# Alternating strides and three-step merges in a dilated attention kernel, with a stepwise memory stage

## The chip, the cores and the metric

The kernel runs on one core of one Trainium2 chip. The metric is device time in microseconds (us) of one launch. A core has TensorE (PE in the profile; PEld is its weight load), VectorE (DVE), ScalarE (ACT), GpSimd (POOL) and SyncE (SP, which here only issues DMAs). DMAs are issued from SP's queue (SPq) or ACT's (ACTq); both feed the same 16 DMA engines.

## The reference

A trunk of two layers over 1024 tokens of width 1024. Layer 0 is dilated sliding-window attention, layer 1 a gated linear recurrence; both also attend to 256 memory tokens. The change concerns layer 0:

```python
h = rms_norm(x, norm_gain[l])
cols = h @ w_in_a[j]                      # q, k, v of 3 groups x 8 heads, memory queries, gate
for g, (window, dil) in enumerate(((128, 1), (512, 4), (2048, 16))):
    o, lse = dilated_window_attention(q[:, :, g], k[:, :, g], v[:, :, g], dil, window // dil)
alpha = softmax(stack(lses), axis=0)      # per token and head, over the groups
mix = sum(alpha[..., None] * stack(outs), axis=0)
kv = rms_norm(mem, mem_gain) @ w_kv       # memory keys and values, both layers
mem_out = softmax(qm @ km^T * scale) @ vm # 4 heads
x = x + (concat([mix, mem_out]) * silu(gate)) @ w_out
```

## The kernel before, in words

Matrices are multiplied in float32 split in two parts: each weight piece (128 x 1024) is loaded as `raw`, then made into `wh` (ACT, rounded) and `wl` (DVE, the rest); a product is three matmuls (high x high, high x low, low x high) of 128 x 128 by 128 x 512. `piece` (L195) does load, high and low part of one piece in one go; `plan` lists all pieces in order, `ahead` prepares them, `take` hands them out. There are two `raw` buffers and four of each of `wh` and `wl`.

Order of the instructions on an engine: a planner orders them by a timing model, except inside `pinned()` (L150), which keeps the written order on the engines it names (TensorE by default). A queue or an engine then runs strictly in the order that the planner left.

Layer 0 runs in these stages:

- Prologue (L1055 to L1074). Four times a pair of x tiles is loaded, normalised, turned and split (`x_pair`), and a projection of gate chunk 0 follows. In the last round come `tables` (L761: sines and cosines of positions, a chain of some 45 small DVE instructions) and the first weight loads `load(0, ...)`, among them block "11"; after that the first split of weights.
- The big projection of q, k and v (`step`, L1037): 252 pinned steps of 12 matmuls, by a seven-product scheme with sums of quarter blocks. `emptied`, `spread`, `normed`, `flip` and `spill_heads` carry each result on over the next seven steps (`BEHIND` = 6) and write it to scratch memory (`qk_scr`, `v_scr`). Scratch rooms in SBUF are `m0` to `m3`, `u0` to `u3`, `w0` to `w3`.
- Its tail and gate slice 0 (L1081 to L1084), in the planner's order.
- Memory stage (L1123 to L1153). The memory tokens are loaded and normalised (`mem_norm`), gate slice 1 runs (`gate_mem`, L1128), the tokens are turned (`mem_turn`), `mem_kv` makes keys and values of both layers (four products of 48 matmuls), then `mem_queries` projects the queries tile by tile and `mem_attend` does scores, softmax and values for pairs of tiles.
- Attention (L1155 to L1277). `heads` lists 12 items (group g, pair of heads hp): four of g = 2 (stride 16), then g = 1 (stride 4), then g = 0 (stride 1). Each has eight steps m: `scores` (L1181 matmuls, L1184 DVE mask and minimum, L1186 ACT exponential with its sum), one step later `turn_` (L1195 transposes, `pts` copy), then `values` (L1208). A step has one key block (g = 2, m < 4 of g = 1, m = 0 of g = 0) or two. Every second step of g > 0 `spill` copies the result to `os` and stores it with two DMAs from ACT's queue (L1228); for g = 0 `merge` (L1231) loads the other two groups' results (`others`), works out the weights from minima and sums in `st`, and stores the weighted sum (L1253). `fetch` loads q, k and v of the next item (1 MB each) on SP's queue, two sets of buffers taking turns. One matmul of gate slices 2 and 3 (`gate_mem_steps`, L533) is put into each step as a filler.
- Gate chunk 1 covers the end of attention; the output projection and layer 1 follow.

At the top, L109 sets the queues: `LQ, SQ, WQ = Y, A, Y`, so loads and weights go by SP (`Y`) and stores by ACT (`A`).

Of the kernel before, what the change touches and what calls it, by code (L numbers as in the profile page):

```python
# [103 lines left out]
def trunk_kernel(ctx, tc, x, mem, pos, norm_gain, w_in_a, q_gain_a, k_gain_a, qk_gain_t, w_out_a,  # L104
# [90 lines left out]
    def piece(src, gain=None):  # L195


        a = src.shape[1]
        raw = rpool.tile([128, 1024], F32, name="raw")
        v = lambda t: t.rearrange("p (a b) -> p a b", a=a)  # L200
        WQ.dma_start(v(raw[:]), src)
# [7 lines left out]
        hi = pool.tile([128, 1024], F32R, name="wh")  # L209
        lo = pool.tile([128, 1024], F32R, name="wl")  # L210
        if gain:
            for b in range(a):
                g = gain()[:, b:b + 1]
                A.activation(v(hi[:])[:, b], v(raw[:])[:, b], AF.Copy, scale=g)
                V.scalar_tensor_tensor(v(lo[:])[:, b], v(raw[:])[:, b], g, v(hi[:])[:, b].bitcast(F32), op0=OP.mult, op1=OP.subtract)
            return v(hi[:]), v(lo[:])
        copy(W_HI, hi[:], raw[:])
        rests.append(W_LO.tensor_tensor(lo[:], raw[:], hi[:].bitcast(F32), op=OP.subtract).ins)  # L218
        return v(hi[:]), v(lo[:])
# [11 lines left out]
    at_piece = [0, 0]  # L231

    def ahead(n):

        while at_piece[1] < min(at_piece[0] + n, len(plan)):
            ready[at_piece[1]] = piece(*plan[at_piece[1]][1:])
            at_piece[1] += 1
# [85 lines left out]
    def mem_gains(pool, name):  # L323

        rows_ = pool.tile([16, 128], F32, name=name)
        Y.dma_start(rows_[:], mem_norm_gain.rearrange("l (k p) -> (l k) p", p=128))
        t = pT.tile([128, 4, 128], F32, name="pt")
        T.transpose(t[:, 0, 0:16], rows_[:], ident[0:16, 0:16])
        V.tensor_copy(memory[0], t[:, 0, 0:16])

    def mem_norm(pool):

        xns = []
        for m in range(2):
            xt = pool.tile([128, D], F32, name="xt")
            Y.dma_start(xt[:], mem[m * 128:(m + 1) * 128, :])
            xns.append(norm_rows(xt[:], None, D, pool))
        return xns

    def mem_turn(pool, xns):  # L340

        mts = []
        for xn in xns:
            hi = pool.tile([128, 8, 128], F32R, name="mhi")
            lo = pool.tile([128, 8, 128], F32R, name="mlo")
            transposed_split(xn, hi, lo, 8)
            mts.append((hi, lo))
        return mts

    def mem_kv(l, mts, pool, put_k, put_v):  # L350


        gt = pool.tile([128, 2], F32, name="mgt")
        Y.dma_start(gt[:], mem_gain_t[l])
        gk = pool.tile([128, 24], F32, name="mgk")
        V.tensor_tensor(gk[:, 0:1], gt[:, 0:1], gt[:, 1:2], op=OP.mult)
        for part in range(2):
            W = take(("mem", l, part), 4)
            pss = [pp.tile([128, 512], F32, name="acc") for _ in range(2)]
            project([ps[:] for ps in pss], [lambda k, t=t: (t[0][:, k, :], t[1][:, k, :]) for t in mts], W)  # L360
            for m, ps in enumerate(pss):
                if part:
                    put_v(m, ps[:])
                else:
                    put_k(m, heads_T(head_norm(ps[:], pool, bufs=1))[:], gk[:, 0:1])

    def mem_queries(key, km, vm, ppool, pool, prob, scr, lhs, before=lambda m: None, after=lambda hp: None):
# [4 lines left out]
        def each(m, ps):  # L372
            t = heads_T(head_norm(ps, pool))
            hi, lo = (pool.tile([128, 4, 128], F32R, name=n, bufs=4) for n in ("qmh", "qml"))
            split_evac(hi[:], lo[:], t[:])
            qs[m] = hi, lo
            before(m)
            if m > 1:
                mem_attend(m // 2 - 1, m % 2, qs, km, vm, ppool, pool, prob, scr)

        project_tiles(key, lhs, each)
        for hp in range(2):
            mem_attend(NT // 2 - 1, hp, qs, km, vm, ppool, pool, prob, scr)
            after(hp)

    def mem_attend(mp, hp, qs, km, vm, ppool, pool, prob, scr):

        ph, pl = (ppool.tile([128, 4, 256], F32R, name=n) for n in ("pmh", "pml"))
        for i in range(2):
# [17 lines left out]
            G.tensor_tensor(p, p, bc(den[:, :, None], [128, 2, MEM]), op=OP.mult)  # L407
            t = pT.tile([128, 4, 128], F32, name="pt")
# [4 lines left out]
            split_evac(ph[:, :, sl], pl[:, :, sl], t[:])  # L413
        o = pO.tile([128, 2, 256], F32, name="po")
# [10 lines left out]
        SQ.dma_start(scr[hp * 256:(hp + 1) * 256, mp * 256:(mp + 1) * 256].rearrange("(h p) t -> p h t", p=128), os[:])  # L425
# [99 lines left out]
    def gate_mem_steps(i):  # L525

        (wh, wl), = take(("gate_m", i), 1)
        for hf in range(2):
# [8 lines left out]
            SQ.dma_start(gatem_scr[i * 128:(i + 1) * 128, hf * 512:(hf + 1) * 512], sg)  # L537
        ahead(4)
# [91 lines left out]
    plan_slices(MG0)  # L630
# [5 lines left out]
    plan_slices(MG1)  # L636
# [101 lines left out]
    with ExitStack() as sa:  # L738
# [19 lines left out]
        def room(name, **kw):  # L758
            return wx.tile([128, 4, 128], F32, name=name, **kw)[:]

        def tables():  # L761

            posi = wx.tile([128, NT], I32, name="w1")
# [885 lines left out]
```

## Time and profile before

| | us |
|---|---|
| median of 3 runs (lowest, highest) | 2116.57 (2115.84, 2116.68) |
| profiled execution, its own time | 2117.12 |
| span of its instructions | 2115.3 |
| first attention scores to the end of attention | about 979 to 1184 |

The profile is of one execution. A line of a group gives the line of the kernel, engine, operation, output and inputs, shapes and count, then busy time, mean time of one, and the idle time of the engine before them with what ended it. A row of a stretch gives busy time per engine, the mean granted TensorE clock (1.00 is full), the share of time that the 16 DMA engines were busy (it can pass 1, since packets overlap) and GB/s. Matmuls are pipelined: the distance of two starts, not the length of one, is its cost.

### The profile page before, as it was taken

How to read it: one execution, taken by the hardware profiler on the slowest of the kernel's cores; microseconds unless marked ns; L12 is line 12 of the kernel's file. 1: busy time of each engine (PE TensorE's matmuls, PEld its weight loads, DVE VectorE, ACT ScalarE, POOL GpSimd, SP SyncE). 2: the span in 40 equal slices, each digit the busy share in tenths (PEclk: the TensorE clock that was granted, in tenths of full speed). 3: DMA queues.
4: the chain of work that ended last, by engine and by line, in shares of the span. 5: the costliest groups of instructions: out<-in, count | busy, mean ns of one | idle time of the engine just before them, and what ended most of it. 6: DMA issues, size and time to landing. Idle time of an engine off the chain costs nothing.

```text
span 2115.3 us, 29553 instructions
## 1 busy us (share of the span) xinstructions
PE 2054.5 (97%) x10713; PEld 1733.5 (82%) x10713; DVE 1242.4 (59%) x2457; ACT 863.1 (41%) x1635; POOL 533.6 (25%) x664
## 2 busy tenths in 40 slices
PE   7899999999999998998898999999999999999999
PEld 6688888888888886787787878888888888888887
DVE  6865566736766465555467554425477762776443
ACT  5454255633554344546566332224522222322220
POOL 3362065703754054122006400012200000000221
PEclk9999999999999999999999999999999999999999
DMA  6277479553544417525899474330301121113643
GB/s 200 93 135 115 130 134 116 120 164 93 119 122 140 130 50 246 185 60 199 276 297 281 147 256 150 125 113 25 100 26 56 57 63 40 51 60 95 234 126 113
DMA packets 418896, 277.21 MB, mean 131 GB/s; under 512 B 220592, under 2 KB 344768, under 8 KB 416704
## 3 DMA queue, kind: packets, MB, share of 16 engines
q1 hardware_dynamic: 379696, 232.20, 40.7%
q10 hardware_dynamic: 39056, 43.14, 5.8%
q8 instruction: 85, 1.39, 0.3%
q14 instruction: 59, 0.48, 0.1%
HBM read 192.32 MB, written 82.97 MB: 130 GB/s over the span
## 4 chain that ended last, share of the span: by engine, by line
PE 46%; DMA 5%; ACT 1%; DVE 1%; issue 0%; ACTq 0%; POOL 0%; SPq 0%; DVEq 0%
PE acc L498 5%; PE acc L499 5%; PE acc L500 5%; PE acc L603 4%; PE acc L604 4%; PE acc L605 4%; PE acc L258 3%; PE acc L256 3%; PE acc L257 3%; DMA o_scr<-os 3%; PE s L1404 1%; PE pt L1404 1%; PE s L1181 1%; PE po L1208 1%; ACT pa L1186 1%; PE pt L299 1%
## 5 line engine op out<-in xcount | busy, mean ns | idle before, releaser
L172 ACT ACTIVATE wh<-raw 128x1024 fp32r<-128x1024 f32 x206 | 216.6, 1054 | 187.0 <-PE acc L499 48.7
L181 POOL TENSOR_TENSOR rr<-rv,nhalf 128x4 f32<-128x4 f32 (+1 forms) x54 | 50.0, 926 | 759.4 <-DVE rv L179 750.9
L1001 POOL TENSOR_TENSOR rr<-rv,nhalf 128x4 f32<-128x4 f32 x96 | 125.0, 1302 | 412.2 <-DVE rv L999 411.0
L889 DVE TENSOR_TENSOR wl<-raw,wh 128x1024 fp32r<-128x1024 f32 x126 | 158.1, 1255 | 115.2 <-ACT wh L172 114.3
L500 PE MATMUL acc<-hhi,wl 128*128 128x512 f32 x480 | 191.4, 399 | 0.1
L498 PE MATMUL acc<-hhi,wh 128*128 128x512 f32 x480 | 190.3, 396 | 1.1 <-ACT wh L172 1.1
L499 PE MATMUL acc<-hlo,wh 128*128 128x512 f32 x480 | 191.3, 398 | 0.0
L218 DVE TENSOR_TENSOR wl<-raw,wh 128x1024 fp32r<-128x1024 f32 x80 | 99.3, 1243 | 131.8 <-ACT wh L172 131.1
L258 PE MATMUL acc<-wh,hlo 128*128 128x512 f32 x384 | 151.0, 394 | 4.9 <-DVE hlo L277 4.9
L256 PE MATMUL acc<-wh,hhi 128*128 128x512 f32 x384 | 150.4, 396 | 1.5 <-ACT wh L172 0.9
L257 PE MATMUL acc<-wl,hhi 128*128 128x512 f32 x384 | 151.0, 393 | 0.0
L603 PE MATMUL acc<-wh,yhi 128*128 128x512 f32 x360 | 142.6, 398 | 0.5 <-ACT yhi L172 0.5
L604 PE MATMUL acc<-wl,yhi 128*128 128x512 f32 x360 | 141.0, 392 | 0.0
L605 PE MATMUL acc<-wh,ylo 128*128 128x512 f32 x360 | 139.8, 393 | 0.0
L957 PE MATMUL acc<-wl,hhi 128*128 128x512 f32 x324 | 127.0, 392 | 4.5 <-DVE wl L889 4.5
L956 PE MATMUL acc<-wh,hhi 128*128 128x512 f32 x324 | 128.1, 395 | 1.6 <-ACT wh L172 1.6
L958 PE MATMUL acc<-wh,hlo 128*128 128x512 f32 x324 | 127.0, 392 | 0.0
L1186 ACT ACTIVATE pa<-pa,st 128x128 f32<-128x128 f32 (+1 forms) x192 | 84.5, 441 | 54.2 <-DVE st L1184 19.4
L498 PEld LDWEIGHTS acc<-hhi,wh 128*128 128x128 f32 x480 | 90.3, 188 | 18.3 <-ACT wh L172 1.6
L499 PEld LDWEIGHTS acc<-hlo,wh 128*128 128x128 f32 x480 | 90.3, 188 | 17.0
L500 PEld LDWEIGHTS acc<-hhi,wl 128*128 128x128 f32 x480 | 90.3, 188 | 16.8 <-DVE wl L218 0.3
L893 DVE TENSOR_TENSOR raw<-raw 128x1024 f32<-128x1024 f32 x72 | 90.2, 1260 | 16.4 <-DMA raw<-in_w_in_a_dram 16.4
(335 smaller groups left out, 5156.5 us busy)
## 6 DMA issues: line engine op xcount, KB each, us to landing
raw<-in_w_in_a_dram SPq DMA_DIRECT2D x115, 512.0 KB, 4.4
raw<-in_w_in_b_dram SPq DMA_DIRECT2D x40, 512.0 KB, 3.7
qk_scr<-m SPq DMA_DIRECT2D x48, 256.0 KB, 3.5
o_scr<-os ACTq DMA_DIRECT2D x96, 128.0 KB, 4.6
raw<-in_w_mem_kv_dram SPq DMA_DIRECT2D x16, 512.0 KB, 3.8
kT<-qk_scr SPq DMA_DIRECT2D x8, 1024.0 KB, 5.3
qT<-qk_scr SPq DMA_DIRECT2D x8, 1024.0 KB, 8.4
vv<-v_scr SPq DMA_DIRECT2D x8, 1024.0 KB, 7.3
```

The source lines that it names most:

```text
L172: A.activation(dst, src, AF.Copy)
L256: T.matmul(ps, hi, wh[:, j, :], start=at == 0, stop=False)
L257: T.matmul(ps, hi, wl[:, j, :], start=False, stop=False)
L258: T.matmul(ps, lo, wh[:, j, :], start=False, stop=at == n - 1)
L498: T.matmul(ps[:], wh[:, k, :], mh, start=k == 0, stop=False)
L499: T.matmul(ps[:], wh[:, k, :], ml, start=False, stop=False)
L500: T.matmul(ps[:], wl[:, k, :], mh, start=False, stop=k == 7)
L603: T.matmul(pss[ch][:], hi[:, k, :], wh[:, j, :], start=first and k == 0, stop=False)
L604: T.matmul(pss[ch][:], hi[:, k, :], wl[:, j, :], start=False, stop=False)
L605: T.matmul(pss[ch][:], lo[:, k, :], wh[:, j, :], start=False, stop=end and k == 3)
L889: V.tensor_tensor(lo[:], source(n, h), hi.bitcast(F32), op=OP.subtract)
L956: T.matmul(flat, hi, wh, start=kt == 0 and p in (0, 1, 5), stop=False, **on)
```

## The change

Four parts of layer 0 are rewritten; layer 1 only gets its memory functions cut up under new names. The arithmetic is the same, but for the merge, whose last product and sum become one instruction per head.

1. **Pieces in parts.** `piece` becomes `piece_raw`, `piece_hi`, `piece_lo`, with `load_piece` and `split_piece` to call them one at a time.
2. **Prologue.** `tables` and the loads of "11" stand ahead of the first gate projection. "11" goes to rooms of the projection's scratch that are unused then; for that, `u2`/`u3` and `w2`/`w3` become halves of one tile each, and `x_pair` uses `u0`, `u1`, `w0`, `w1` only.
3. **Memory stage.** Loads, norm and turning of the memory tokens, and loads and splits of the pieces needed, are put into the last steps of the big projection. Its eight tail steps, now with TensorE pinned, take 12 matmuls each of gate slice 0 and of the memory keys. The other three key/value products follow. Queries run in 13 pinned rounds; gate slice 1 moves from before the key/value products into the last five of them.
4. **Attention.** The items alternate; q and k are fetched two items ahead (three sets), v one ahead; fillers come three at a time in stride 16 alone; stores in attention and in the memory stage go by SP; the `os` buffers are three, in a pool of their own; `merge` is split into `weigh`, its `rest` and `merge`, which run in successive steps.

Its core:

```diff
@@ prologue
         W = take(("gate", 0), 4)
+        tables()
+        for h in range(2):
+            load(0, "11", h)
         for j in range(4):
...
-                tables()
...
-                for b, h in (("11", 0), ("11", 1), ("12", 0), ("12", 1), ("21", 0), ("21", 1), ("22", 0)):
+                for b, h in (("21", 1), ("21", 0), ("12", 0), ("12", 1), ("22", 0)):
                     load(0, b, h)
@@ end of the projection
+        def memory_ahead(k):
+            if k == LAST - 11:
+                for m in range(2):
+                    xms.append(wraw.tile([128, 1024], F32, name="raw")[:])
+                    mem_load(m, xms[m])
+            if k in (LAST - 8, LAST - 7):
+                mem_norm(xms[k - LAST + 8], wraw.tile([128, 1024], F32, name="raw")[:])
...
+            if at in (-2, -1, 2, 3):
+                split_piece(1)
+            if at in (-3, -2, 1, 2):
+                split_piece(0)
+            if at in (-6, -5, -1, 0, 3):
+                load_piece()
...
-        step(LAST + 1)
-        gate_mem(MG0[0], between=lambda: [step(LAST + k) for k in (2, 3, 4)])
-        for k in range(5, BEHIND + 3):
-            step(LAST + k)
+        ahead_of = memory_steps()
+        for k in range(1, BEHIND + 3):
+            with pinned():
+                if k in (3, 4):
+                    mts.append(mem_turn(k - 3))
+                for _ in range(96 // (BEHIND + 2)):
+                    next(ahead_of)
+                step(LAST + k, lambda: pieces(LAST + k))
@@ memory queries
-            mem_queries("qmem_a", km, vm, *mp, ...)
+            cover = gate_mem_steps(MG0[1])
+            for m in range(NT + 5):
+                with pinned():
+                    if m < NT:
+                        acc = pp.tile([128, 512], F32, name="acc")
+                        project([acc[:]], [lhs_natural(m)], W, ...)
+                        normed_[m] = head_norm(acc[:], mattn, bufs=2)
+                    else:
+                        for _ in range(10):
+                            next(cover, None)
+                    if later:
+                        later.pop(0)()
+                    if m - 5 in turned_:
+                        mem_values((m - 5) // 2, (m - 5) % 2, turned_.pop(m - 5), vm, om_scr)
+                    if m - 4 in shown:
+                        turned_[m - 4] = mem_turned(shown.pop(m - 4), mprob)
+                    if m - 1 in normed_:
+                        qs[m - 1] = mem_query(normed_.pop(m - 1), mattn)
+                    if 3 <= m < NT + 3:
+                        shown[m - 3] = mem_scores((m - 3) // 2, (m - 3) % 2, qs, km, prob)
@@ attention
-        heads = [(g, hp) for g in (2, 1, 0) for hp in range(4)]
+        heads = [(2, 0), (1, 0), (2, 1), (1, 1), (0, 0), (2, 2), (1, 2), (0, 1), (2, 3), (1, 3), (0, 2), (0, 3)]
...
+            pool, n = (rooms_[1], 2) if at % 3 else (rooms_[0], 1)
...
+            spool = s1.enter_context(tc.tile_pool(name="spill", bufs=3, reuse_waits="tile"))
...
-                    SQ.dma_start(group_rows(o_scr[g][hp // 2], g, m - 1 + i)[:, hp % 2 * 256:hp % 2 * 256 + 256],
+                    Y.dma_start(group_rows(o_scr[g][hp // 2], g, m - 1 + i)[:, hp % 2 * 256:hp % 2 * 256 + 256],
...
-                V.tensor_tensor(y[:], o[:], wg(0), op=OP.mult)
-                V.tensor_tensor(y[:], y[:], og[0], op=OP.add)
+                for j in range(4):
+                    V.scalar_tensor_tensor(y[:, j], o[:, j], w0[:, j // 2, j % 2:j % 2 + 1], og[:, j], op0=OP.mult, op1=OP.add)
...
-                        next(fill, None)
+                        for _ in range(3 if g == 2 else 0):
+                            next(fill, None)
+                        if soon:
+                            soon.pop()()
                         if turned:
                             values(*turned.pop())
+                        if rest:
+                            rest.pop()()
+                        before = scored[-1] if scored else None
+                        if before and before[0] == 0 and before[2] % 2:
+                            rest.append(weigh(before[1], before[2] - 1))
+                        if g == 1 and hp % 2:
+                            {0: load_piece, 6: lambda: split_piece(0), 7: lambda: split_piece(1)}.get(m, lambda: None)()
+                        if g == 0 and m % 2:
+                            others(hp, m - 1)
+                        if m == 0:
+                            fetch_qk(at + 2)
+                        if m == 3:
+                            fetch_v(at + 1)
```

More of the change, by code (lines that the diff above doesn't have):

```diff
@@ L209, in piece, with piece_lo @@
         hi = pool.tile([128, 1024], F32R, name="wh")
+        if gain:
+            for b in range(a):
+                A.activation(v(hi[:])[:, b], v(raw[:])[:, b], AF.Copy, scale=gain()[:, b:b + 1])
+        else:
+            copy(W_HI, hi[:], raw[:])
+        return pool, hi
+    def piece_lo(pool, hi, raw, src, gain=None):
+        a = src.shape[1]
+        v = lambda t: t.rearrange("p (a b) -> p a b", a=a)
         lo = pool.tile([128, 1024], F32R, name="wl")
@@ L321, in trunk_kernel @@
     memory = []
[L323 to L365, printed above, removed]
+    def mem_load(m, to):
+        Y.dma_start(to, mem[m * 128:(m + 1) * 128, :])
@@ new lines, in mem_norm, with mem_part @@
+    def mem_norm(xt, junk):
+        ss = small.tile([128, 1], F32, name="ss1")
+        A.activation(junk, xt, AF.Square, accum_out=ss[:])
+        r = rsqrt(ss[:], 1, D)
+        V.tensor_scalar(xt, xt, r[:], None, op0=OP.mult)
+    def mem_part(l, part, mts):
+        W = take(("mem", l, part), 4)
+        pss = [pool.tile([128, 512], F32, name=n)[:] for pool, n in ((pp, "acc"), (pO, "po") if part else (pp, "acc"))]
+        for i, (wh, wl) in enumerate(W):
+            for ps, (h, l_) in zip(pss, mts):
+                for j in range(2):
+                    at = 2 * i + j
+                    for lhs, w in ((h, wh), (h, wl), (l_, wh)):
+                        T.matmul(ps, lhs[:, at, :], w[:, j, :], start=at == 0 and lhs is h and w is wh, stop=at == 7 and lhs is l_)
+                        yield
+            ahead(1 + i)
+        return pss
@@ L536, in gate_mem_steps @@
             twice_silu(sg, ps[:])
[L537 to L538 removed]
+            Y.dma_start(gatem_scr[i * 128:(i + 1) * 128, hf * 512:(hf + 1) * 512], sg)
+        if further:
+            ahead(4)
     def out_proj(key, load, load_x, y_T, x1, finish, pool, before, by_tile=False):
@@ L1159, in trunk_kernel @@
             rooms_[1] = ap_
-            pairs, turned = {}, {}
+            pairs, weighed, soon = {}, {}, []
+            near = {}
             def others(hp, m):
-                got = []
+                got = near[hp, m] = []
                 for g in (1, 2):
@@ L1257, in fillers @@
                 for i in MG1:
-                    yield from gate_mem_steps(i)
+                    yield from gate_mem_steps(i, False)
             fill = fillers()
-            fetch(1)
-            scored, turned = [], []
+            scored, turned, rest = [], [], []
+            fetch_qk(1)
             for at, (g, hp) in enumerate(heads):
-                if at and at + 1 < len(heads):
-                    fetch(at + 1)
                 for m in range(NT):
```

248 lines of the change are left out of this document (178 added, 70 removed).

## The prediction

> **What bounds the kernel now.** I read the first page, then busy time by stage, then who TensorE waits for, then the order of time at the places where it waits.
>
> ```profile
> span 2115.3 us, 29553 instructions
> PE 2054.5 (97%) x10713; PEld 1733.5 (82%) x10713; DVE 1242.4 (59%) x2457; ACT 863.1 (41%) x1635; POOL 533.6 (25%) x664
> ```
>
> TensorE (PE) is busy for 2054.5 of 2115.3 us, so only 60.8 us of idle time can be taken away, plus time that the busy figure hides: matmuls at the half clock, and matmuls that start later than they could. The change leaves the matmuls themselves alone. So the question is where the 60.8 us lie, and whether the edits reach them. By stage (columns: stretch, its length, PE, PEld, DVE, ACT, POOL busy, granted clock, DMA share, GB/s):
>
> ```profile
> 0.00:84.00 84.00, 62.44 (x271) 48.94 (x272) 63.17 (x99) 45.03 (x77) 29.43 (x28) 0.96 0.56 178
> 796.00:901.00 105.00, 95.92 (x445) 77.47 (x444) 56.98 (x94) 51.13 (x81) 27.29 (x45) 0.97 0.69 219
> 901.00:979.00 78.00, 72.77 (x446) 63.35 (x445) 46.00 (x101) 40.97 (x108) 24.63 (x24) 1.00 0.23 68
> 979.00:1037.00 58.00, 48.67 (x347) 44.94 (x346) 27.42 (x159) 33.79 (x141) 0.00 (x0) 0.91 0.85 290
> 1037.00:1101.00 64.00, 60.47 (x437) 54.80 (x436) 36.89 (x163) 41.43 (x150) 0.00 (x0) 1.00 0.92 293
> 1101.00:1184.00 83.00, 77.46 (x530) 69.17 (x529) 67.15 (x250) 52.59 (x180) 52.83 (x45) 1.00 0.81 255
> ```
>
> The rows are: the prologue; the end of the big projection with the memory keys and values; the memory queries; and attention at stride 16, at stride 4 and at stride 1. Length minus PE gives idle time of 21.6, 9.1, 5.2, 9.3, 3.5 and 5.5 us, together 54.2 of the 60.8. All six stages are touched by the change. What ends the idle time (three more waits, of 6.6, 4.5 and 1.6 us, stand in rows further down, with the wait in brackets):
>
> ```profile
> PE po L1208 <- ACT os L172: 8.8, 5, 2.9
> PE pt L821 <- DVE xt L291: 7.8, 1, 7.8
> PE pt L1195 <- ACT pa L1186: 5.8, 5, 2.4
> PE acc L258 <- DVE hlo L277: 4.9, 4, 2.0
> PE po L420 <- ACT pmh L172: 2.4, 2, 1.6
> PE pt L411 <- DVE qml L277: 1.2, 1, 1.2
> PE acc L498 <- ACT wh L172: 1.1, 1, 1.1
> ```
>
> The numbers behind the colon are total, times and longest. The 7.8 us are the first load of x, which nothing here can shorten. The rest are the change's targets.
>
> **Part 1, the prologue.** `tables` and the two loads of block "11" move ahead of the first gate projection, and the first split of weights no longer waits for them.
>
> ```profile
> L786 DVE TENSOR_TENSOR w<-w 128x128 f32<-128x128 f32 x12 | 4.6, 381 | 0.3
> L785 DVE TENSOR_SCALAR w<-w 128x128 f32<-128x128 f32 x13 | 2.9, 225 | 0.3
> 78.07 1.22 DVE L889 TENSOR_TENSOR wl<-raw,wh 128x1024 fp32r<-128x1024 f32 x1
> 74.34 0.50 PE L956 MATMUL acc<-wh,hhi 128*128 128x512 f32 x1 [1.63 <-ACT wh L172]
> 79.35 0.80 PE L957 MATMUL acc<-wl,hhi 128*128 128x512 f32 x1 [4.51 <-DVE wl L889]
> 79.94 0.63 PE L958 MATMUL acc<-wh,hlo 128*128 128x512 f32 x1
> 80.37 0.63 PE L956 MATMUL acc<-wh,hhi 128*128 128x512 f32 x1
> ```
>
> The chain of tables (4.6 + 2.9 us in its two largest groups) sits on DVE just before the low part `wl` at 78.07, for which PE waits 4.5 us. The next matmuls start 0.43 us apart (79.94, 80.37) where 0.23 is usual (rows of part 3), about seven of them, 1.4 us. To be gained: 1.6 + 4.5 + 1.4, and the 2.0 us wait on `hlo` that fell among the tables: 9.5 us. Against it: the 7.5 us of tables now compete with the second pair of x tiles, on a DVE that is busy 63.2 of 84 us and that PE already waited for in each gate projection; and 1.05 MB of weights (two loads of 512 KB) go ahead of that pair in the sync queue, at 178 GB/s 5.9 us. Only pinned sections fix the order; here the planner chooses, so the tables fall into gaps or in front. Bounds: a gain of 9.5, a loss of 7.5 + 5.9 - 9.5 = 3.9. I take the middle, rounded up since DVE has 20.8 us free: **gain 5**.
>
> **Part 2, memory stage.** Loading, normalising and turning of the memory tokens move into the last steps of the projection; gate slice 0 and the four key/value products run between those steps, 12 matmuls a step; the queries become rounds, each working on five tiles at different points; gate slice 1 covers the last five rounds.
>
> ```profile
> 842.93 1.94 PE L299 MATMUL pt<-ident,xn 128*128 128x128 f32 x8 [6.62 <-DVE rv L179]
> 840.00:860.00 20.00, 17.07 (x74) 14.16 (x75) 9.61 (x18) 9.13 (x16) 2.13 (x3) 0.83 0.68 243
> 855.61 27.06 SPq L201 DMA_DIRECT2D raw<-in_w_mem_kv_dram  x10
> ```
>
> The 6.6 us wait for the normalised tokens goes, since the tokens are then ready 11 steps earlier. So does its half clock: 20 us at 0.83 is 3.4 us short, of which the time before 842.93 was idle anyway; I count 2. The 1.1 us for gate weights (L498) goes. Of the waits in the last query rounds (2.4 + 1.2) I count half, 1.8: with ten filler matmuls (2.3 us) a round the chain of maximum, exponential, scaling and turning is still longer than the cover. Together 11.5. What is late next is the weight supply: ten loads took 27.06 us, 2.7 us a piece, and a piece feeds 12 matmuls of 0.23, 2.7 us. There is no slack, and any pinned wait adds up: I charge 0.5. The stores that move to the sync queue here (om, gatem and kv scratch, 256 KB each) have nobody waiting near. **Gain 11**; bounds 14.3 (all idle time of both rows) and a loss of 2, if the fixed order costs a wait of 1 us, the size of the present ones, in each of 13 rounds.
>
> **Part 3, attention.** Order of heads 16, 4, 16, 4, 1, ...; three fillers a step in stride 16 alone instead of one everywhere; q and k fetched two heads ahead; three store buffers instead of two; stores on the sync queue; merge in three steps.
>
> ```profile
> 817.02 0.60 PE L316 MATMUL pt<-ident,w 128*128 128x128 f32 x4
> 817.38 0.48 PE L498 MATMUL acc<-hhi,wh 128*128 128x512 f32 x1
> 817.69 0.40 PE L499 MATMUL acc<-hlo,wh 128*128 128x512 f32 x1
> 817.92 0.40 PE L500 MATMUL acc<-hhi,wl 128*128 128x512 f32 x1
> ...
> 1162.98 0.61 PE L1181 MATMUL s<-kT,qT 128*128 128x128 f32 x4
> 1163.43 0.60 PE L1195 MATMUL pt<-ident,pa 128*128 128x128 f32 x4
> 1163.79 0.48 PE L533 MATMUL acc<-hlo,wh 128*128 128x512 f32 x1
> 1164.10 1.05 PE L1208 MATMUL acc<-vv,pts 128*128 128x128 f32 x8
> 1164.99 1.03 PE L1181 MATMUL s<-kT,qT 128*128 128x256 f32 x4
> 1165.86 0.60 PE L1195 MATMUL pt<-ident,pa 128*128 128x128 f32 x4
> ```
>
> Read starts, not lengths. The first 512-column matmul behind transposes takes 0.31 us (817.38 to 817.69), the next 0.23; a lone filler takes 0.31 (1163.79 to 1164.10). So 96 lone fillers pay the 0.08 extra 96 times, 32 groups of three 32 times: 64 x 0.08 = 5.1 us saved. A step with one key block needs about 1.08 us of PE (scores 0.45; transposes and values half of a two-block step's, 0.18 and 0.45), one with two blocks 0.87 + 0.35 + 0.89 = 2.1.
>
> ```profile
>   ACT os L172: 10.9, 10
> DMA to landing us min/median/max: 1.9/4.4/9.6
> L1228 ACTq DMA_DIRECT2D o_scr<-os x64: 326/356/925, 986.2 to 1108.8; - x64
> L1186 ACT ACTIVATE pa<-pa,st 128x128 f32<-128x128 f32 x64 | 25.0, 392 | 17.4 <-DVE st L1184 7.9 <-DMA qT<-qk_scr 4.3 <-DVE pts L174 3.7
> ```
>
> At stride 16 a step was 1.08 + 0.31 = 1.39 us of PE, so two store buffers last 2 x 2 x 1.39 = 5.6 us, and stores took 4.4 in the median and up to 9.6 to land: ACT waited 10.9 us for them and PE for ACT (8.8). With three fillers a step is 1.08 + 0.77 = 1.85 us and three buffers last 11. So most of the 9.3 us idle goes; I count 7. The clock there was 0.91, 58 x 0.09 = 5.2 us short, partly while PE idled: I count 4. The issue of stores leaves ACT, 64 at 0.36 us, which matters only where ACT is the longest. Sum 5 + 7 + 4 = 16. Stride 4 loses its fillers, so ACT, with two exponentials of 0.39 and their read-outs, becomes longer than PE's 1.08 us in the one-block steps: 16 steps by about 0.25, minus 4. Stride 1 loses its fillers too, 32 x 0.31 = 10 of 83 us; DVE's 67.2 us then stand against 73, so of the 5.5 idle little goes, in spite of earlier loads for the merge: plus 3. **Gain 15**; bounds 28 (idle 18.3, clock 5.2, fillers 5.1) and a loss, priced below.
>
> **Sum.** 5 + 11 + 15 = 31 us. The profiled execution took 2117.1 us (span 2115.3); the median of the runs is 2116.57, 0.5 lower. 2117.1 - 31 - 0.5 = 2085.6, so **2086**.
>
> **The rivals.** *Stores stuck in the sync queue (slower).* Loads and stores now share one queue, in order. A fetch of q and k is 2.1 MB, at 290 GB/s 7.2 us. A store issued behind it lands after 4.4 + 7.2 = 11.6 us. Three buffers last 6.5 us in the one-block steps of stride 4 (3 x 2 x 1.08), so each of two pairs there would wait 5.1 us, in four heads 41 us: 2086 + 41 = 2127. It decides once landing passes 6.5 us. [...] Against it in the trace: fetches come once in eight steps, and the pairs with the shortest steps come when the fetch at step 0 is 3 steps old. Chance 0.10.
>
> *The order moves the waits (smaller gain).* Tables land ahead of the second pair, the fixed PE order in the memory rounds eats what it saves, and attention alone gains: 2117 - 15 = 2102. For it: DVE 63 of 84 us, a weight supply with no slack. Chance 0.22.
>
> *All reachable idle time goes.* 9.5 + 14.3 + 28 = 52 us: 2065. For it: engines other than PE are under 80% nearly everywhere; DMA needs 290 GB/s x 205 us = 59 MB in some 178 us, 334 GB/s, above the 290 reached, which speaks against. Chance 0.15.
>
> *The transfers bound attention.* 59 MB at the 293 GB/s of the stride-4 row is 203 us, today's length, and only parts 1 and 2 gain: 2101. That share was 0.92 and not full, so it is mild; chance 0.05, and it lies in the range.
>
> **How the numbers follow.** Forecast 0.48, with its own range 2074 to 2098 (half of each term's distance to its bounds). Of the five cases, four are faster by more than 0.2% (4.2 us, about what a measurement of this kernel tells from no change). Allowing 0.04 of the smaller gain to end within 0.2% gives faster 0.86, same 0.04, slower 0.10. The range leaves out the slow rival and the tip of the best case: 2062 to 2112.
>
> **What would show it.** In the profile after: no wait of `wl` L889 near 79 us and PE idle under 17 us in the prologue (part 1 right); no L299 wait for memory tokens, no half clock around it, key/value products gapless between steps (part 2); attention some 190 us long, fillers in groups with 0.23 us starts, and no ACT wait on `o_scr<-os` above a few us (part 3). The forecast is wrong if store landing in attention has a median above 6.5 us with PE waiting on ACT's `os`, if the second gate projection starts 7 us later than now, or if a stage's PE busy time falls with no shorter stretch.

## The result, and the profile after

The changed kernel takes 2097.87 us (median of 4 runs, 2093.66 to 2100.98) against 2116.2 us (4 runs of the kernel before beside it): ratio 0.9915, 95% interval 0.9897 to 0.9932. The profiled execution took 2098.17 us, with a span of 2096.4. The kernel is faster by 18 us and not by the forecast's 31; 2097.9 lies at the edge of the forecast's own range and nearer to the time of the rival "the order moves the waits" (2102).

The page of the changed kernel, its span and its busy times:

```profile
span 2096.4 us, 29609 instructions
PE 2049.9 (98%) x10713; PEld 1732.3 (83%) x10713; DVE 1231.3 (59%) x2489; ACT 863.3 (41%) x1635; POOL 527.4 (25%) x664
```

TensorE's idle time went from 60.8 to 46.5 us. Busy time by stage, columns as before (prologue; end of the projection with keys and values; queries; then attention in three stretches):

```profile
0.00:79.00 79.00, 61.86 (x263) 48.84 (x263) 59.40 (x103) 47.88 (x80) 28.62 (x28) 0.96 0.55 174
801.00:876.00 75.00, 72.71 (x342) 58.97 (x341) 49.42 (x79) 40.53 (x66) 23.49 (x34) 1.00 0.68 207
876.00:974.00 98.00, 88.72 (x511) 76.56 (x510) 47.40 (x101) 44.28 (x111) 24.37 (x24) 0.97 0.28 91
974.00:1029.00 55.00, 53.20 (x390) 49.08 (x389) 33.64 (x163) 38.22 (x145) 0.00 (x0) 1.00 1.00 353
1029.00:1083.00 54.00, 45.79 (x333) 41.45 (x332) 29.55 (x154) 32.76 (x121) 13.06 (x12) 1.00 0.93 304
1083.00:1163.00 80.00, 77.16 (x564) 71.13 (x563) 57.35 (x273) 56.01 (x199) 30.92 (x29) 1.00 0.86 273
```

Two rows stand out: the queries (876 to 974) are idle for 9.3 us, more than before (5.2), and the second stretch of attention, with the first stride-1 head in it, for 8.2. Who TensorE waits for, after:

```profile
PE pt L857 <- DVE xt L321: 7.9, 1, 7.9
PE pt L346 <- DVE pml L307: 7.5, 5, 3.4
PE acc L288 <- DVE hlo L307: 6.1, 3, 2.4
PE po L1361 <- ACT os L172: 4.3, 3, 2.8
PE acc L996 <- DVE wl L928: 1.2, 1, 1.2
PE acc L286 <- ACT wh L172: 0.8, 1, 0.8
```

The waits for the memory tokens (6.6 us) and most of `wl` (4.5) are gone. `hlo` has grown (4.9 before) and L346, the turning of the memory queries, is new. Stage ends, read from four starts (the last group of three projection matmuls, the first scores, the last values, the last matmul of the program):

| stage | before | after | gain | forecast |
|---|---|---|---|---|
| to the last projection matmul | 808.65 | 805.85 | 2.8 | 5 |
| from there to the first scores | 171.2 | 168.6 | 2.6 | 11 |
| first scores to last values | 226.8 | 215.2 | 11.6 | 15 |
| from there to the last matmul | 904.5 | 902.5 | 2.0 | 0 |

Nothing of the last row was changed; it lies between 902.3 and 904.1 us in all the other kernels below, so its 2.0 us are about what executions differ by.

**Half-clock windows.** One thing must be read before these numbers are used. The granted clock drops to 0.5 in stretches of 3.41 us, called half windows below. Matmuls of 128x512 start 0.43 us apart in the one at 46.01 us and 0.23 us apart behind it, so each window costs up to 1.7 us, half its length, if TensorE could have been busy in all of it. These are four pairs of neighbouring stretches of the changed kernel (same columns):

```profile
42.60:46.01 3.41, 1.02 (x8) 0.59 (x6) 3.41 (x4) 1.15 (x4) 3.41 (x3) 1.00 0.50 154
46.01:49.42 3.41, 3.41 (x8) 2.73 (x9) 2.58 (x5) 1.47 (x3) 1.70 (x2) 0.50 0.21 79
59.61:63.02 3.41, 1.08 (x7) 0.63 (x5) 2.89 (x3) 2.30 (x5) 3.41 (x3) 1.00 0.00 0
63.02:66.43 3.41, 3.36 (x8) 2.69 (x9) 1.19 (x2) 1.19 (x2) 1.76 (x2) 0.50 0.23 80
871.99:875.40 3.41, 1.81 (x7) 0.93 (x6) 1.23 (x1) 1.54 (x2) 0.00 (x0) 1.00 0.94 230
875.40:878.81 3.41, 3.41 (x12) 2.71 (x11) 0.85 (x2) 1.28 (x2) 0.31 (x1) 0.50 0.97 366
936.90:940.31 3.41, 0.49 (x5) 0.24 (x3) 2.62 (x5) 2.54 (x5) 1.01 (x1) 0.99 0.66 202
940.31:943.72 3.41, 2.97 (x14) 2.97 (x15) 3.33 (x5) 1.62 (x2) 0.00 (x0) 0.50 0.69 190
```

In each pair TensorE is busy for 0.49 to 1.81 of 3.41 us, and the next stretch runs at half clock with PE busy nearly throughout. Ahead of the program's last instructions there are four such windows after the change (up to 6.8 us lost) and seven before (up to 11.9 us), so up to 5.1 of the 18.9 us by which the last matmul comes earlier are clock. All starts lie on one grid of 3.413 us, whose phase differs from execution to execution. That matters for every comparison below.

### The profile page after: what moved, and what is told of

It reads as the page before. It is cut to its first block, busy times and chain, and to the rows that moved or that the text cites. A ratio compares the mean times of both kernels' runs of the same rounds, so it can differ in the third digit from the quotient of the medians.

```text
span 2096.4 us, 29609 instructions
## 1 busy us (share of the span) xinstructions
PE 2049.9 (98%) x10713; PEld 1732.3 (83%) x10713; DVE 1231.3 (59%) x2489; ACT 863.3 (41%) x1635; POOL 527.4 (25%) x664
## 4 chain that ended last, share of the span: by engine, by line
PE 89%; DVE 4%; DMA 3%; ACT 2%; issue 2%; POOL 1%; SPq 0%; DVEq 0%; ACTq 0%; POOLq 0%
PE acc L997 7%; PE acc L996 7%; PE acc L995 7%; PE acc L527 5%; PE acc L528 5%; PE acc L529 5%; PE acc L633 4%; PE acc L634 4%; PE acc L635 4%; PE acc L288 3%; PE acc L287 3%; PE acc L286 3%; PE pt L346 2%; PE po L995 2%; PE po L997 2%; PE po L996 2%
## 5 line engine op out<-in xcount | busy, mean ns | idle before, releaser
L928 DVE TENSOR_TENSOR wl<-raw,wh 128x1024 fp32r<-128x1024 f32 x122 | 152.8, 1253 | 112.5 <-ACT wh L172 112.0
L529 PE MATMUL acc<-hhi,wl 128*128 128x512 f32 x448 | 178.7, 399 | 0.0
L528 PE MATMUL acc<-hlo,wh 128*128 128x512 f32 x448 | 178.5, 398 | 0.0
L527 PE MATMUL acc<-hhi,wh 128*128 128x512 f32 x448 | 177.6, 396 | 0.0
L230 DVE TENSOR_TENSOR wl<-raw,wh 128x1024 fp32r<-128x1024 f32 x80 | 99.8, 1251 | 118.3 <-ACT wh L172 112.3
L1339 ACT ACTIVATE pa<-pa,st 128x128 f32<-128x128 f32 (+1 forms) x192 | 84.7, 442 | 51.0 <-DVE st L1337 50.2
L528 PEld LDWEIGHTS acc<-hlo,wh 128*128 128x128 f32 x448 | 84.3, 188 | 15.7
L527 PEld LDWEIGHTS acc<-hhi,wh 128*128 128x128 f32 x448 | 84.3, 188 | 15.6
L529 PEld LDWEIGHTS acc<-hhi,wl 128*128 128x128 f32 x448 | 84.3, 188 | 15.4
L932 DVE TENSOR_TENSOR raw<-raw 128x1024 f32<-128x1024 f32 x68 | 85.2, 1262 | 16.7 <-DMA raw<-in_w_in_a_dram 16.6
```

Source lines behind the costliest of these rows:

```text
L527: T.matmul(ps[:], wh[:, k, :], mh, start=k == 0, stop=False)
L528: T.matmul(ps[:], wh[:, k, :], ml, start=False, stop=False)
L529: T.matmul(ps[:], wl[:, k, :], mh, start=False, stop=k == 7)
```

## The experiments

All times, with the ratio to the kernel before on the same chip, and three marks of the profiled execution: last projection matmul, first scores, last values. Beside the kernels from the third row on, the kernel before took 2114.3 to 2114.7 us and not 2116.2, so kernels are better compared by their ratios than by their medians; 0.001 is 2.1 us. The changed kernel has two ratios, 0.9915 and 0.9926.

| kernel | median us | ratio, 95% interval | proj. | scores | values | half windows |
|---|---|---|---|---|---|---|
| before | 2116.2 | 1 | 808.7 | 979.9 | 1206.7 | 7 |
| changed | 2097.9 | 0.9915, 0.9897 to 0.9932 | 805.9 | 974.5 | 1189.7 | 4 |
| changed, again | 2097.3 | 0.9926, 0.9909 to 0.9942 | 806.1 | 974.4 | 1188.4 | 5 |
| stores on ACT | 2110.0 | 0.9984, 0.9973 to 0.9995 | 804.4 | 972.5 | 1200.9 | 4 |
| before, stores on sync | 2109.0 | 0.9982, 0.9971 to 0.9992 | 807.7 | 979.4 | 1199.6 | 5 |
| two store buffers | 2105.3 | 0.9961, 0.9951 to 0.9972 | 805.9 | 972.8 | 1199.8 | 5 |
| old order of heads | 2099.6 | 0.9931, 0.9914 to 0.9948 | 804.6 | 971.7 | 1194.3 | 5 |
| one filler a step | 2093.9 | 0.9909, 0.9889 to 0.9929 | 805.3 | 974.0 | 1185.8 | 7 |
| fillers in stride 1 | 2102.3 | 0.9951, 0.9932 to 0.9970 | 805.8 | 972.8 | 1193.3 | 6 |
| queries turned first | 2094.8 | 0.9912, 0.9892 to 0.9933 | 806.0 | 967.4 | 1184.5 | 4 |
| tables last | 2096.0 | 0.9917, 0.9896 to 0.9937 | 804.2 | 971.2 | 1185.9 | 2 |
| tables and loads last | 2096.1 | 0.9917, 0.9902 to 0.9933 | 806.3 | 974.6 | 1188.9 | 5 |
| queries first, tables last | 2097.2 | 0.9918, 0.9902 to 0.9933 | 807.5 | 972.1 | 1188.8 | 5 |
| the same, one filler | 2094.7 | 0.9908, 0.9888 to 0.9928 | 809.7 | 974.3 | 1188.1 | 8 |

The theory that the two traces suggested was that attention is held up by the sync queue, that the queries' new wait comes from two PSUM buffers for turned tiles, and that the tables' work was moved and not removed.

**The queue of the stores.** The four attention stores go back to ACT:

```diff
-                    Y.dma_start(group_rows(o_scr[g][hp // 2], g, m - 1 + i)...
+                    SQ.dma_start(group_rows(o_scr[g][hp // 2], g, m - 1 + i)...
```

> The changed kernel with the attention stores (spilled rows, statistics, merged rows) back on ACT's queue; all else as changed (2097.9 us). Theory 'the sync queue is the bottleneck at the start of attention': each transfer in it is issued only once one about eight places earlier has landed (waits of 3.1, 1.9 and 1.7 us stand at 1017 to 1033 us), so with 76 stores fewer the statistics loads for head (0,0), issued at 1031 to 1033 us, go out 3 us earlier, (0,0) falls from 22.0 us by about 3 and (2,2) from 19.9 by about 2: 2092 to 2094 us, with ACT waiting for stores 1 to 3 us as now. Rival 'POOL's chain sets the stalls': no change in (0,0) and (2,2), 2097 to 2099. Rival 'the issue of stores on ACT was a cost': 76 issues of some 0.36 us return to ACT, 27 us of its time, and where ACT is the longest engine (stride 4) some 4 to 8 us come back: 2102 to 2106.

It came out 12 us slower than the changed kernel by the medians and 12 to 15 by the ratios, which is more than any of the three expected, and the first theory fell. The head (1,0) takes 18.9 us instead of 12.8, and (0,1) and (0,2) take 19.9 and 20.5 instead of 16.5. ACT's waits in attention show why (who waited, for whom, total, times, longest):

```profile
ACT pa L1339 <- DMA vv<-v_scr: 6.2, 1, 6.2
ACT pa L1339 <- issue: 3.5, 2, 3.1
ACT pa L1339 <- DMA qT<-qk_scr: 2.6, 1, 2.6
ACT pa L1339 <- DMA kT<-qk_scr: 2.1, 1, 2.1
```

The exponential at L1339 reads none of these. What stands ahead of it on ACT does, as the order of time shows:

```profile
985.83 4.73 ACTq L1381 DMA_DIRECT2D o_scr<-os  x2
990.61 0.40 ACT L1339 ACTIVATE pa<-pa,st 128x128 f32<-128x128 f32 x1 [6.16 <-DMA vv<-v_scr]
991.16 0.86 PE L1348 MATMUL pt<-ident,pa 128*128 128x128 f32 x2 [4.22 <-ACT pa L1339]
```

The two issues themselves take 0.33 us each; the second begins 4.4 us behind the first. In the traces before and after, the 787 transfers of each program use eight completion semaphores in turn (767 of the 779 repeated uses after come exactly eight transfers behind the one before), and none was issued before the last transfer on its semaphore had landed. The second store here uses the one of a `vv` load issued at 977.8, and it is issued when that load has landed, at 990.2. On ACT the exponential behind it waits (6.16 us), and TensorE for that (4.22). In the changed kernel such waits stand in the sync queue, the longest of them 3.1 us, and `pa` waits for no transfer at all. In the profile before, such waits add up to 4.3 + 4.2 + 4.0 us (`pa` for `qT`, `o_scr`, `og`). The first of them is of the same kind: the store ahead of it, issued at 1013.44, uses the semaphore of a `qT` load that landed at 1013.42.

```profile
ACT pa L1186 <- DMA qT<-qk_scr: 4.3, 1, 4.3
ACT pa L1186 <- DMA o_scr<-os: 4.2, 1, 4.2
ACT pa L1186 <- DMA og<-o_scr: 4.0, 1, 4.0
```

Does the move pay alone? The same edit in the kernel before:

```diff
-                    SQ.dma_start(group_rows(o_scr[g][hp // 2], g, m - 1 + i)...
+                    Y.dma_start(group_rows(o_scr[g][hp // 2], g, m - 1 + i)...
```

> The kernel before with one edit: the four attention stores go to the sync queue; order of heads, fillers, two store buffers and merge as before (2116.6 us). Theory 'a store on ACT's queue holds up the exponentials behind it whenever the transfers fall behind, and the new order makes them fall behind': before, issues took 0.33 to 0.93 us, 0.36 in the median, so only the issue itself is saved, and ACT's wait for the two buffers (10.9 us) stays: 2110 to 2117. Rival 'the queue alone earns it': the 12 us that its undoing cost in the changed kernel come here too, 2103 to 2106. Rival 'stuck behind the fetches': stores land later than two buffers allow, 2120 to 2130.

2109.0 us, and attention 220.3 us instead of 226.8. The 5.8 us that TensorE waited for `pa` at L1195 are gone; its wait for `os`, and ACT's for the two buffers (12.4 us), stay. So the move earns about 4 us alone by the ratio (2 to 6 by its interval). The stage shows 6.6, of which up to 3.4 are clock (three half windows in attention before, one here). In the new arrangement it earns 12 to 15, and there transfers are denser (DMA share 1.00, 353 GB/s in the first stretch of attention, against 0.85 and 290). The first theory of this run was right about what stays, and by the ratio (0.9982 of 2116.6 is 2112.8) also about the time; that only the issue itself would be saved was too low. The rivals fail.

Landing hardly suffered: the issue rows of the changed kernel and of the one with stores on ACT (last column: median us to landing).

```profile
o_scr<-os SPq DMA_DIRECT2D x96, 128.0 KB, 5.1
```

```profile
o_scr<-os ACTq DMA_DIRECT2D x96, 128.0 KB, 4.9
```

A queue apart from the loads is worth 0.2 us of landing to the stores here, and costs 12 to 15 us of time.

**The store buffers.**

```diff
-            spool = s1.enter_context(tc.tile_pool(name="spill", bufs=3, reuse_waits="tile"))
+            spool = s1.enter_context(tc.tile_pool(name="spill", bufs=2, reuse_waits="tile"))
```

> The changed kernel with two store buffers instead of three. Theory 'three buffers took away the waits of ACT for landing stores' (10.9 us of ACT, 8.8 of TensorE before): landing is 5.1 us in the median and up to 9.6, a pair takes 3.7 us at stride 16 and 2.2 to 2.6 at stride 4 with one block, so waits come back at stride 4 above all: ACT 6 to 10 us, time 2102 to 2106. Rival 'the longer steps of stride 16 alone removed them': ACT's wait stays under 3 us and the time within 1.5 us of 2097.9.

2105.3 us, 7 to 10 slower by medians and ratios, with ACT's wait for landing stores back, and larger than the 6 to 10 us expected:

```profile
ACT os L172 <- DMA o_scr<-os: 23.3, 16, 3.6
```

It was 0.9 us in the changed kernel. The third buffer is what removed it; the rival fails.

**The order of heads.**

```diff
-        heads = [(2, 0), (1, 0), (2, 1), (1, 1), (0, 0), (2, 2), (1, 2), (0, 1), (2, 3), (1, 3), (0, 2), (0, 3)]
+        heads = [(g, hp) for g in (2, 1, 0) for hp in range(4)]
```

> The changed kernel with the old order of heads: all of stride 16, all of stride 4, all of stride 1 (the last weight slice for the fillers is split two heads later). Theory 'the order earned the gain, since it spreads transfers and merges': attention goes back towards its old 205 us from first scores to last values, 2107 to 2113. Rival 'fillers in threes, three store buffers and the steps of the merge earned it': stride 16 keeps 4 x 14.8 = 59 us, stride 4 4 x 12.5 = 50 us, stride 1 is held by transfers of 6.3 MB a head at 353 GB/s, 17.8 us, 71 us together: 180 us against 188.4 from first to last scores now, and (0,0), which need no longer run just behind the first spills, loses its 22.0: 2088 to 2092.

(The last weight slice for the fillers is also split at other heads, as the old order needs.) 2099.6 us: neither. Stride 16 (58.5 us for four heads) and stride 4 (52.8) came as the rival said, but stride 1 took 84.5 and not 71, since four heads of merges in a row wait for the loads of the other strides (POOL for `og` 17.2 us, 3.5 in the changed kernel) and TensorE for the merge:

```profile
PE po L1361 <- DVE os L1413: 10.4, 4, 3.4
```

Attention is 7.3 us longer than in the changed kernel, of which four half windows (none there) account for up to 6.8; the ratios (0.9931 against 0.9915 and 0.9926) have intervals that overlap. What the order alone earns is not settled.

**The fillers.** One in each step of attention, and, in another kernel, three in each step of stride 1:

```diff
-                        for _ in range(3 if g == 2 else 0):
+                        for _ in range(1):
```

```diff
-                        for _ in range(3 if g == 2 else 0):
+                        for _ in range(3 if g == 0 else 0):
```

> The changed kernel with one filler in every step of attention instead of three in each step of stride 16. Theory 'a lone filler behind transposes starts 0.08 us late': 64 more such starts, 5.1 us, and stride 16 with steps of 1.39 us instead of 1.85 asks for transfers faster than they come: 2103 to 2107. Rival 'fillers in stride 1 and 4 cover the merge and the transfers': (0,0) and (2,2), 22.0 and 19.9 us now, come down together by 4 or more, and the time is within 2 us of 2097.9 or below.

> The changed kernel with the three fillers a step in stride 1 instead of stride 16. Theory 'transfers and the merge chain set the stalls': a head of stride 1 moves 6.3 MB and needs POOL 14 us, in 16.5 us of TensorE; with fillers it has some 19 us for both, and stride 16 (4.2 MB) 12.7: rates of 330 and 331 GB/s even out, (0,0) stays near 22 instead of 22 plus 4.4, (2,2) and (2,3) fall to 13 to 15: 4 to 8 us faster, 2090 to 2094. Rival 'the pairs of stride 16 need the time for their stores': ACT waits for stores return, as before the change, 8 us or more: 2100 to 2106.

The extra cost of a lone filler is there. In order of time, the changed kernel and the one with single fillers:

```profile
1003.28 0.48 PE L562 MATMUL acc<-hhi,wh 128*128 128x512 f32 x1
1003.59 0.39 PE L562 MATMUL acc<-hlo,wh 128*128 128x512 f32 x1
1003.82 0.40 PE L562 MATMUL acc<-hhi,wl 128*128 128x512 f32 x1
1004.06 0.38 PE L1361 MATMUL po<-vv,pts 128*128 128x128 f32 x2
```

```profile
1076.14 0.47 PE L562 MATMUL acc<-hhi,wh 128*128 128x512 f32 x1
1076.45 0.61 PE L1361 MATMUL po<-vv,pts 128*128 128x128 f32 x4
```

0.31 us for the first after transposes, 0.23 for the next two. Yet attention with single fillers takes 211.8 us, not more than the changed kernel's 215.2, and the time is 2093.9. The intervals of the ratios (0.9909 against 0.9915 and 0.9926) overlap, so a gain is not shown, but the loss that the theory forecast is not there, and the rival holds. Undisturbed heads of stride 1 take 18.32 instead of 16.48 us, but (2,2) takes 13.0 instead of 19.9 and (2,3) 12.7 instead of 18.1. Stalls also come elsewhere: (1,0) and (1,1) take 17.3 and 20.3 us instead of 12.8 each. With the fillers in stride 1, the time is 2102.3. Its stride-1 heads take 22.05 us without a stall, while stride 16, with no filler left, still takes 12.5 us a head and more, not the 8.6 that its matmuls need (first head): 4.2 MB in 12.5 us is 336 GB/s, close to the 353 of the first stretch of attention in the changed kernel. So the rival's time came, but not by its mechanism, since ACT waits for stores only 1.7 us. That the transfers set the pace there is likely and not shown: in (2,1), from 1000.0 to 1012.4 us, the DMA share is 1.06 at 382 GB/s, but TensorE's only listed wait is 1.7 us for `os`. Where the fillers stand decides which stalls they cover; that they serve as time for the transfers is a reading of these two runs.

**The memory queries.**

```diff
+                    if m - 1 in normed_:
+                        qs[m - 1] = mem_query(normed_.pop(m - 1), mattn)
                     if m - 5 in turned_:
...
-                    if m - 1 in normed_:
-                        qs[m - 1] = mem_query(normed_.pop(m - 1), mattn)
```

> The changed kernel with the turning of the new queries moved ahead of the values and of the turning of the probabilities in each round of the memory queries. Theory 'two PSUM buffers for turned tiles': the probabilities take both, and the queries' turning right behind them needs one that the low part on DVE has just begun to read; waits of TensorE for it at L346 are 7.5 us, with a half clock window of 3.4 us (1.7 us lost). With 24 to 36 matmuls between, those waits go: 4 to 8 us faster, 2090 to 2094, and the stage 876 to 974 us becomes some 5 to 8 us shorter. Rival 'the wait passes on': the values wait for the turned probabilities or the probabilities' turning for the buffers, and the stage keeps its length within 1.5 us: 2096.5 to 2098.

From the last projection matmul to the first scores 161.5 us instead of 168.6, and no half window in it instead of two: 7.2 us, as the theory said of the stage, of which up to 3.4 are clock. The mechanism in the changed kernel, in order of time, first TensorE and then DVE:

```profile
936.35 1.04 PE L435 MATMUL pt<-ident,pm 128*128 128x128 f32 x8
940.75 0.48 PE L346 MATMUL pt<-ident,qn 128*128 128x128 f32 x1 [3.36 <-DVE pml L307]
```

```profile
938.27 1.23 DVE L230 TENSOR_TENSOR wl<-raw,wh 128x1024 fp32r<-128x1024 f32 x1 [0.76 <-ACT wh L172]
939.41 0.68 DVE L340 TENSOR_TENSOR qn<-acc,rr 128x512 f32<-128x512 f32 x1
940.01 1.28 DVE L307 TENSOR_TENSOR pml<-pt,pmh 128x512 fp32r<-128x512 f32 x2
```

The turning of the probabilities (eight transposes) takes both buffers of turned tiles; the queries' turning comes right behind it and gets its buffer only when DVE has formed `pml`, and DVE was busy with a weight split. With the queries first, the wait at L346 for `pml` is gone, but the probabilities now wait:

```profile
PE pt L435 <- POOL pm L424: 3.9, 7, 1.9
PE pt L435 <- DVE rv L179: 2.2, 2, 1.6
```

So of 9.2 us (L346 7.5, L435 1.7) 3 are gained and 6.1 remain, at places that open no half window in that execution. The whole kernel took 2094.8 us. By the ratio (0.9912 against 0.9915 and 0.9926) that is a gain of 1 to 3 us, which the intervals do not tell from none; attention was 1.9 us longer, with two half windows where the changed kernel had none.

**The prologue.** Tables behind the last pair of x tiles (with other scratch rooms for them), early loads kept:

```diff
         W = take(("gate", 0), 4)
-        tables()
         for h in range(2):
             load(0, "11", h)
...
             else:
+                tables()
                 s0.close()
```

> The changed kernel with the position tables back behind the last pair of x tiles; the two early weight loads stay early. Theory 'the tables' DVE time is moved, not removed': ahead they make TensorE wait for hlo three times (6.1 us) and halve the clock twice; behind they delay the low part of the first weights again. The waits for hlo fall to some 2 us, the wait for wl at 77 to 80 us returns with 3 to 4.5 us and its half clock: 2099 to 2102 (2 to 4 us slower). Rival 'the early loads alone did it': wl is then ready in spite of the tables and the hlo waits go: 2093 to 2095, 3 to 5 us faster.

and with the two loads behind it as well:

```diff
-        for h in range(2):
-            load(0, "11", h)
...
-                for b, h in (("21", 1), ("21", 0), ("12", 0), ("12", 1), ("22", 0)):
+                for b, h in (("11", 0), ("11", 1), ("21", 1), ("21", 0), ("12", 0), ("12", 1), ("22", 0)):
```

> The changed kernel with both prologue edits undone: tables behind the last pair of x tiles, and the loads of block '11' behind it too. Theory 'the early loads earn the prologue's gain and the early tables give part of it back': with the tables alone undone the last projection matmul came at 804.2 us (changed 805.9, before 808.7), so with both undone it comes back to 807.5 to 809, with waits for wh or wl of 4 to 6 us at 72 to 80 us; time 2099 to 2102. Rival 'the weights' split no longer waits for the tables, whenever the loads come': last projection matmul at 804 to 805.5, time 2095 to 2097.

2096.0 and 2096.1 us: neither edit of the prologue earns anything that can be measured, and the second run speaks against the theory that the early loads do (2099 to 2102 was expected by it). Its last projection matmul, at 806.3 us with two half windows in the prologue, lies between the two forecasts. The waits trade places: with tables last, `hlo` 3.4 us and `wl` 2.4; as changed, 6.1 and 1.2.

**Together, and the yardstick.** Queries first and tables last, then with single fillers in addition, beside the changed kernel again:

> The changed kernel itself once more, as the yardstick for the three beside it and for how much the stages of one program differ between executions: 2096 to 2100 us; last projection matmul at 805.5 to 806.5 us, first scores at 972.5 to 975, (0,0) and (2,2) again 20 us or more each.

> The changed kernel with two of the edits above together: query turning ahead in each memory round, tables last (early loads kept). Theory 'they lie in different stages and add up': 7.2 us in the memory queries, 1.7 in the prologue, 9 together: 2088 to 2090. Rival 'attention's arrangement answers to what comes before it' (with the first edit alone it became 1.9 us longer, so that 4.3 of the 7.2 arrived): 2091 to 2094.

> The kernel beside it with, in addition, one filler in every step of attention instead of three in stride 16. Theory 'lone fillers cost some 4 us of TensorE, but the covered steps of stride 4 and 1 lose fewer stalls': attention was 211.8 us from first scores to last values instead of 215.2, so 3 us faster than its neighbour: 2085 to 2088. Rival 'where the stalls fall is decided anew by every edit': attention 213 to 218 us, and no gain over its neighbour.

2097.3, 2097.2 and 2094.7 us: the edits do not add up, and no version is shown to beat the changed kernel. One reason shows in the traces. The order of TensorE's matmuls in the prologue is the same with tables last as in these two combinations, and the last projection matmul comes at 804.2, 807.5 and 809.7 us. The first has no half window in the prologue, the second two, the third four. Around the same wait in the first and the third:

```profile
39.39:42.80 3.41, 2.09 (x14) 1.53 (x12) 2.84 (x5) 3.41 (x8) 1.84 (x2) 1.00 0.53 173
42.80:46.21 3.41, 2.03 (x8) 1.39 (x9) 2.85 (x3) 1.87 (x4) 3.41 (x3) 1.00 0.17 67
```

```profile
40.40:43.81 3.41, 1.59 (x6) 0.68 (x5) 2.97 (x4) 3.15 (x8) 2.87 (x3) 1.00 0.71 195
43.81:47.22 3.41, 2.38 (x7) 1.86 (x7) 2.85 (x5) 1.09 (x2) 3.41 (x3) 0.50 0.13 40
```

In the first the idle time is split over two windows of the grid (2.09 and 2.03 us busy) and costs nothing more; in the third it falls mostly into one (1.59), and the next is slow. Stage ends of single executions therefore differ by up to 5.5 us here, and the query turning's 7.2 us were 3.7 in the combinations (164.6 against 168.3 in the repeat).

## Why the prediction was right or wrong

**Right:** the sign, that the time lies in the range, that attention earns most, that the token wait, its half clock and ACT's wait for `o_scr<-os` go, that attention comes near 190 us (188.4 from first to last scores, 199.8 before), that landing in attention stays under 6.5 us (5.1 in the median, where the slow rival had 11.6) so that the slow rival does not happen, and that the weight supply is next (0.8 and 0.8 us of waits and a half window at 875).

**What was too high.** Of the 31 us, 19 came at the last matmul and 18 in the time: part 1 missed 2.2 us, part 2 8.4 (the largest) and part 3 3.4, and 2.0 came from a stage that nothing changed. What happened is told better by the rival "the order moves the waits" (chance 0.22) than by the forecast: waits for `hlo` behind the early tables, a fixed order in the memory rounds that eats most of what it saves, and attention as the main gain. That the time still falls into the forecast's own range is in part luck. Half of each term's distance to its bounds, as the prediction words it, gives 2076 to 2097 when part 3's loss is left out, and not 2074 to 2098.

**Part 1 (5 us).** The step that failed is that early tables and loads shorten the prologue. The middle of the bounds, 9.5 and -3.9, is 2.8 and not 5; it was rounded up because DVE had 20.8 us free. DVE was not free at the moments that counted: with the tables beside the second pair, the waits for `hlo` are 6.1 us, and two of them opened half windows. The profiles show 2.8 us, but with both edits undone the time is the same, so this agreement with the middle is luck. The `wl` wait was 2.4 us there and not the 4.5 of before; what else in the new prologue shortened it was not tried. The 1.4 us counted for matmuls that start 0.43 us apart were half clock (0.5 from 76.0 to 82.8 us), and two half windows are still in the prologue, at 46 and 63 us. Its idle time is 17.1 us, just above the 17 that the prediction named.

**Part 2 (11 us).** The token wait of 6.6 us went, and so did the two half windows beside it (840.6 to 847.4 us). The step that failed is the price of a fixed order: a wait of 1 us in each of 13 rounds stood only as the lower bound. It was five waits of 7.5 us together and a half window behind the longest, with a place that could have been named: two buffers of turned tiles, taken by the probabilities just ahead of the queries' turning. With the half window at 875 the stage has two again, so the 2 us counted for clock are not there on balance. Measured 2.6 in the profile. One row was misread: 27.06 us for ten weight loads is the time over which they were issued. Each landed 3.5 to 4.6 us after its issue, and for 16.4 us of the stretch the queue waited for `wl` to free a buffer, so it is the pace of that chain and not of the transfers.

**Part 3 (15 us).** The size was close (11.6 in the first profile, 12.8 in the repeat), but the terms were not. Store buffers: 7 counted, 7 to 10 measured. Clock: 4 counted; up to 5.1 us of half windows fell away in one execution and 3.4 in the other. Fillers: the 0.08 us is there, the 5.1 us of gain is not; with lone fillers attention was not longer. The step that failed most is that issuing stores from ACT matters only where ACT is the longest engine: counted at nothing, it measures about 4 us alone and 12 to 15 together. The row that said so was quoted: of 17.4 us of idle time before `pa` at L1186, 4.3 ended with `qT`, which `pa` does not read.

The single undoings in attention (queue 13.1 us of stage time, buffers 11.8, order 7.3) sum to 32 us where the whole earned 11.6. Without 1.7 us for each half window of the longer kernel (2, 2, 4, and 3 in the kernel before) it is still 18.6 against 6.5. So the edits are worth more when the others are there; that a late store or load then finds nothing to cover it is the likely reason and was not tried.

**Where the rest is.** In the changed kernel (0,0) takes 22.0 and (2,2) 19.9 us, against 16.5 for the next stride-1 heads and 14.5 for stride 16 in the run with the old order. The trace reads as a chain in (0,0):

```profile
1042.15 4.03 POOL L1403 TENSOR_TENSOR og<-og,mw 128x512 f32<-128x512 f32 x4 [71.47 <-DMA o_scr<-os]
1046.14 2.49 POOL L1404 TENSOR_TENSOR og<-og,og 128x512 f32<-128x512 f32 x2
1047.44 1.13 DVE L1413 SCALAR_TENSOR_TENSOR os<-acc,mw,og 128x128 f32<-128x128 f32 x4 [4.23 <-POOL og L1404]
1048.94 0.51 ACT L1339 ACTIVATE pa<-pa,st 128x256 f32<-128x256 f32 x1 [5.44 <-DVE st L1337]
1050.07 0.60 PE L1361 MATMUL acc<-vv,pts 128*128 128x128 f32 x3 [1.86 <-ACT pts L172]
```

Two pairs are weighed at once, POOL does four products before the first sum, DVE's merge stands ahead of the next mask and waits 4.2 us, and the exponential and TensorE wait in turn. This is argued from the trace and was not tried by itself.

## What to carry to other kernels

Look for an instruction that waits for a transfer it does not read: here a DMA issue stood ahead of it in its engine's queue, and moving such issues, of 0.33 us each, to an engine with nothing else to do was worth 12 to 15 us, and about 4 us as the only edit. When several uses of a small set of buffers are put in a row by a fixed order, count the buffers against the uses before counting the gain. And compare the number of half-clock windows before comparing stage times of two executions; a few microseconds (up to 1.7 us a window here) may be nothing but where a wait fell on the grid.

## What the runs showed of the hardware that was not expected

The half windows lie on a grid of 3.413 us, to within 0.01 us in each of 14 profiled executions, with a phase of its own in each (windows start 0.92 us past a multiple of it before, 1.61 after). Between 20 and 2050 us, every one of the 45 windows in which TensorE was busy for less than 0.40 was followed by one at half clock (five of them before, three after); from 0.40 to 0.50 it was 17 of 32, from 0.50 to 0.62 4 of 39 (busy shares are modelled, so a window or two at each edge may belong to the neighbour). The other six of the 72 half windows followed one with 0.65 to 0.80 that was itself at half clock. The two in the prologue of the changed kernel stand behind waits of 2.4 us for `hlo`.
